# Layer 0's background adaLN sums: two of eight k tiles moved from VectorE to TensorE, and a new pace

## The chip, the cores and the metric

The kernel runs on one core of one Trainium2 chip. Its time is the device time of one execution in microseconds. A core has TensorE (PE, the matmuls; PEld are its weight loads), VectorE (DVE), ScalarE (ACT), GpSimd (POOL) and SyncE (SP), which here issues every load. The engines run side by side, each through its own queue in order, and wait for one another by semaphores.

## The reference

Two layers of a diffusion trunk run over 256 context tokens and 256 latent tokens, 1024 channels wide. For each layer:

```
sh1, sc1, ga1, sh2, sc2, ga2 = split(silu(c) @ mod_w + mod_b, 6)     # adaLN, one vector per stream
h = rms_norm(x) * g1 * (1 + sc1) + sh1
lx, ly, gq, ..., bg = split(h @ w_in)
y1, y2, y3 = rglru(lx, ly), gla(gq, gk, gv, gr, gz), gqa(aq, ak, av)
x = x + ga1 * ((sigmoid(bg1)*(y1@wb1) + sigmoid(bg2)*(y2@wb2) + sigmoid(bg3)*(y3@wb3)) @ w_out)
x = x + ga2 * (relu((rms_norm(x)*g2*(1+sc2) + sh2) @ w1)**2 @ w2)
```

`mod_w` is 1024 x 6144 in each layer. The product `silu(c) @ mod_w` has only two rows, one for the context and one for the latent stream, and it gives the 48 columns of 128 that the kernel keeps in `modT`.

## The kernel before, in words

All activations lie with channels on the partitions, in eight k tiles of 128 channels by 512 tokens. A weight tile (512 KB) is loaded by SP into one of three `wraw` buffers, split by ACT (`wh`, L200) and DVE (`wl`, L201) into a high and a low part (three buffers of each), and used in 24 matmuls (`gemm`, L252: eight k tiles by three products). Before each k tile `gemm` calls `tick()`.

The text calls a vector sum over `mod_w` an adaLN sum. The six sixths of `mod_w` are numbered u = 0 to 5; each is done in two halves of 512 columns. For layer 0, u = 0 and 1 are done at the start (`mod_half`, straight on TensorE). The generator `mods` (L310) does u = 2 to 5, that is eight halves, behind other work. For a half it loads eight tiles t of 128 x 512 (256 KB each, L319), and for each of them multiplies t by the conditioning scalar of its partition and adds it to an accumulator, once for each of the two streams: ACT for k = 0 (L339), DVE for k = 1 to 7 (L341). What remains is a sum over 128 partitions, which `mod_cols` (L288, here called the close of a half) does on TensorE: the accumulators are multiplied by `pick`, a 128 x 32 matrix with a single column of ones, in four column strips. The result is copied, transposed and added to its bias; this last part, `turn()`, comes only when the next half is closed. So both halves of u are done once the first half of u + 1 is closed.

`mods` gives a number at each step, and the kernel's own pacing clock (L206 to L231) decides at which `tick()` the next step is written into the program: every matmul advances this clock by its columns / 2400 (four times that for plain f32), so a gemm of 512 tokens counts 5.12 units and one of 256 tokens 2.56; a step is due the given number of units after the one before. `need(l, u)` (L245) writes all the steps that are missing until u is done, at once, without matmuls between them.

The stretch in question, in program order: `spawn(mods(0, range(2, 6), ...))` (L916); eleven `merge` calls of two gemms each at 512 tokens; `need(0, 2)` (L924); eight out-projection gemms on tokens 0 to 255, each followed by a `residual` on DVE (L933); the norm statistics of that half; `need(0, 3, 4)` (L953) and `norm_apply` of that half; eight out-projection gemms on tokens 256 to 511, statistics and `norm_apply` again; the first five tiles of `up` for each half of the tokens, three for all 512; `need(0, 5)`; then `mods(1, ...)` is spawned for layer 1.

`tmp()` tiles of 128 x 512, which the loads, the accumulators and the norms share, come from a pool of 10 buffers. The compiler's list scheduler orders each engine's queue; `tc.high_priority(n)` moves an instruction up by n places in it (300 for the loads of `mods`, 800 for the weights and for the norms).

Of the kernel before, what the change touches and what calls it, by code (L numbers as in the profile page):

```python
# [23 lines left out]
KT = 8  # L24
# [13 lines left out]
GZP, G0P = 2, 6  # L38
AHEAD = 800
L_SM, L_PT = 4.0, 1.5  # L40
M_A, M_K, M_S = 300, 3.0, 2.0
NDVE = (0, 2, 5)
NL = 2
O_LX, O_LY, O_GQ, O_GK, O_GV, O_GR, O_GZ = 0, 1024, 2048, 2560, 3072, 4096, 5120
# [60 lines left out]
def trunk_kernel(ctx: ExitStack, tc: tile.TileContext, out: bass.AP, d: dict):  # L105
# [17 lines left out]
    def tmp():  # L123
        return t2.tile([128, 512], F32, name="t2")
# [4 lines left out]
    def tmp1(dt=F32, shape=(128, 256)):  # L129
        return t1.tile(list(shape), dt, name="t1")  # L130
# [10 lines left out]
    def mx():  # L141
        return ps_mx.tile([128, 512], F32, name="mx")
# [6 lines left out]
    cs = const.tile([128, KT, 32], F32, name="cs")  # L149
# [14 lines left out]
    pick = const.tile([128, 2, 32], F32, name="pick")  # L164
# [4 lines left out]
    def pc(l, name, a=0, n=None):  # L169
        lo, hi = PCOLS[name]  # L170
        return par[:, l, lo + a:hi if n is None else lo + a + n]
# [38 lines left out]
    def mm(o, a, b, **kw):  # L210
        clock[0] += b.shape[-1] * (4 if b.dtype == F32 else 1) / 2400
        P.matmul(o, a, b, **kw)  # L212

    def tp(o, a):
        clock[0] += a.shape[-1] * 2 / 2400
        P.transpose(o, a, ident)  # L216
# [16 lines left out]
    def spawn(gen):  # L233
        tasks.append([clock[0], gen])

    def finish(done=lambda: not tasks):

        while not done():
            t = min(tasks, key=lambda t: t[0])
            clock[0] = max(clock[0], t[0])  # L240
            step(t)
# [3 lines left out]
    def need(l, *us):  # L245
        finish(lambda: all((l, u) in done for u in us))
# [41 lines left out]
    def mod_cols(l, n, terms, nk, dsts):  # L288

        ps = mx()  # L290
        for k in range(nk):
            w, r = terms(k)
            for j in range(4):
                mm(ps[32 * j:32 * j + 32, :n], w, r(n * j), start=k == 0, stop=k == nk - 1)
        sb = tmp1()
        S.copy(sb[:, :n], ps[:, :n])
        yield 0.0
        pt = mx()
        m = n // 128
        for i in range(m):  # L300
            tp(pt[:, 128 * i:128 * i + 128], sb[:, 128 * i:128 * i + 128])

        src = pt[:, :n].rearrange("p (i j b) -> p j i b", i=m, j=4)[:, :, :, 0:2]
        q = 4 // len(dsts)
        for h, o in enumerate(dsts):
            dst = modT[l][:, o:o + q * m, :].rearrange("p (j i) b -> p j i b", j=q)
            bia = pc(l, "modb", o, q * m).rearrange("p (j i) -> p j i", j=q).unsqueeze(3).to_broadcast([128, q, m, 2])
            V.tensor_tensor(dst, src[:, q * h:q * h + q], bia, op=ALU.add)

    def mods(l, us, pace):  # L310

        halves = [(u, j) for u in us for j in range(2)]

        def load(u, j, k):
            with tc.high_priority(M_A):
                t = tmp()
                nc.sync.dma_start(t, d["mod_w"][l, u][:, k, 512 * j:512 * j + 512])  # L319
            return t  # L320

        def turn():
            if last:
                for _ in last[0]:
                    pass
                if last[2]:
                    done.add((l, last[1]))

        last = None
        for u, j in halves:  # L330
            bs = (0, 1) if l == 0 or u < 2 else (1,)
            acc = [tmp() for _ in bs]
            nx = load(u, j, 0)
            for k in range(KT):
                t, nx = nx, load(u, j, k + 1) if k + 1 < KT else None
                for a, b in zip(acc, bs):
                    c = cs[:, k, b:b + 1]
                    if k == 0:
                        S.activation(a, t, AF.Copy, scale=c)  # L339
                    else:  # L340
                        V.scalar_tensor_tensor(a, t, c, a, op0=ALU.mult, op1=ALU.add)  # L341
                yield pace
            yield M_S
            g = mod_cols(l, 128, lambda i, acc=acc, bs=bs: (pick[:, bs[i], :], lambda c: acc[i][:, c:c + 128]),
                         len(bs), (4 * u if j == 0 else 8 + 4 * u,) if u < 2 else (8 * u + 4 * j,))
            next(g)
            turn()
            last = g, u, j
        yield pace
        turn()  # L350
# [110 lines left out]
    for l in range(NL):  # L461
# [305 lines left out]
        def merge(b, i, yh, yl):  # L767
            pb = gemm(weight(l, "br", b, i), yh, yl, c0)
            pg = gemm(weight(l, "in", O_BG + 1024 * b + 128 * i), hh, hl, c0)
            g = gtmp()  # L770
            S.activation(g[:, c0:], pg, AF.Tanh, scale=0.5)  # L771
            if b == 0:
                V.scalar_tensor_tensor(m[:, i, :], g[:, c0:], 1.0, pb, op0=ALU.add, op1=ALU.mult)
            else:
                V.scalar_tensor_tensor(g[:, c0:], g[:, c0:], 1.0, pb, op0=ALU.add, op1=ALU.mult)
                V.tensor_tensor(m[:, i, :], m[:, i, :], g[:, c0:], op=ALU.add)
            if b == 2:
                split_to(mh[:, i, c0:], ml[:, i, c0:], m[:, i, :])
# [34 lines left out]
        for t, ps in gemm_tok(l, O_AK, hh, hl, range(4)).items():  # L813
# [4 lines left out]
            a = tmp1()  # L818
# [25 lines left out]
        def gqa_q(j):  # L844

            qT = []
            ssq = sm.tile([128, 4, 4 - t0], F32, name="ssq")
            qss = {}
            for t, pq in gemm_tok(l, O_AQ + 512 * j, hh, hl, range(t0, 4)).items():
                for g in range(2):  # L850
                    ps = pq[:, 256 * g:256 * g + 256]
                    q = tmp1()
                    for a in range(2):
                        S.activation(q[:, 128 * a:128 * a + 128], ps[:, 128 * a:128 * a + 128], AF.Square,
                                     accum_out=ssq[:, 2 * g + a, t - t0:t - t0 + 1])
                    if t < 2:
                        S.copy(q, ps)
                    else:
                        rope(q, ps, 0, t - 2)
                    qss[g, t] = q  # L860
            for g in range(2):
                for a in range(2):
                    pt = mx()
                    for t in range(t0, 4):
                        P.transpose(pt[:, 128 * t:128 * t + 128], qss[g, t][:, 128 * a:128 * a + 128], ident)
                    q = tmp()
                    if not last:
                        S.activation(q[:, :256], pt[:, :256], AF.Copy, scale=pc(l, "qg"))
                    S.copy(q[:, 256:], pt[:, 256:])
                    qT.append(q)  # L870
            rs = sm.tile([128, 4, 4 - t0], F32, name="rsq")
            rsqrt(rs.rearrange("p a b -> p (a b)"), ssq.rearrange("p a b -> p (a b)"), 1.0, 128.0 * EPS)
            return qT, rs
# [31 lines left out]
        for st_ in QORD[l]:  # L905
            if st_ == "q":
                qs[len(qs)] = gqa_q(len(qs))
            elif st_ in "01":
                for g in ((0, 1), (2, 3)):
                    spawn(attend(int(st_), g, *qs[int(st_)]))  # L910
            elif st_ == "f":
                finish()
            elif st_ == "m":
                merge(1, next(mi), y2h, y2l)
            elif st_ == "u" and l == 0:
                spawn(mods(0, range(2, 6), M_K))  # L916
        if l:
            finish()
        mh, ml = ytiles("yh")
# [52 lines left out]
        for c in range(5):  # L972
            if c < 4:
                hid[c] = ytiles(("yh", "yl")[c % 2])
                n = NSPL if c == 0 and not last else 0
                for a, b in halves:
                    for i in range(n):
                        up(c, i, a, b)
                for i in range(n, 8):
                    up(c, i, c0, T)  # L980
            if c == 0:
                need(l, 5)
            if c == 4 and not last:
                need(1, 0, 1)
                hn1 = norm_mul(l + 1, 1)
                for a, b in halves[::-1]:
                    for i in range(8):
                        down(3, i, a, b)
                    with tc.high_priority(NHP):
                        norm_apply(l + 1, 1, x, a, b, norm_stats(x, a, b), hn1, range(8))  # L990
            elif c > 0:
                for i in range(8):
                    down(c - 1, i, c0, T)
                    if c == 4:
                        nc.sync.dma_start(out[:, i, :], x[:, i, 256:])
            if l == 0 and c == 0:
                spawn(mods(1, range(5), 1.5 * M_K))
        x1 = x


# [101 lines left out]
```

## Time and profile before

| | |
|---|---|
| median of 3 runs | 1927.91 us (1926.07 to 1928.13) |
| profiled execution, its own time | 1926.13 us |
| its span, first to last instruction | 1924.3 us |
| PE, DVE, ACT busy | 95%, 66%, 48% of the span |
| mean granted TensorE clock | 0.98 of full |

An engine's busy share is an average over the whole span. Where TensorE is busy without a break, what the other engines do is hidden; where it is idle, the profile names what ended the wait.

### The profile page before, as it was taken

How to read it: one execution, taken by the hardware profiler on the slowest of the kernel's cores; microseconds unless marked ns; L12 is line 12 of the kernel's file. 1: busy time of each engine (PE TensorE's matmuls, PEld its weight loads, DVE VectorE, ACT ScalarE, POOL GpSimd, SP SyncE). 2: the span in 40 equal slices, each digit the busy share in tenths (PEclk: the TensorE clock that was granted, in tenths of full speed). 3: DMA queues.
4: the chain of work that ended last, by engine and by line, in shares of the span. 5: the costliest groups of instructions: out<-in, count | busy, mean ns of one | idle time of the engine just before them, and what ended most of it. 6: DMA issues, size and time to landing. Idle time of an engine off the chain costs nothing.

```text
span 1924.3 us, 27716 instructions
## 1 busy us (share of the span) xinstructions
PE 1819.8 (95%) x10696; PEld 1544.4 (80%) x10696; DVE 1273.0 (66%) x2137; ACT 926.4 (48%) x1586; POOL 58.0 (3%) x88
## 2 busy tenths in 40 slices
PE   5998999999999999779999999996999999999999
PEld 4765778887777888778888889764888878999999
DVE  5677764445566984889854448787765677566665
ACT  3778544343443333454332325877654554445442
POOL 1000000000000000010000000000000000000000
PEclk9999999999999999879999999998999999999999
DMA  9322223222221653847643236531433333664654
GB/s 313 99 74 69 68 71 97 76 90 77 66 66 45 224 170 124 271 130 235 209 133 99 93 94 191 159 124 62 129 120 114 123 115 98 240 182 148 186 180 150
DMA packets 91619, 255.66 MB, mean 133 GB/s; under 512 B 9184, under 2 KB 20576, under 8 KB 91488
## 3 DMA queue, kind: packets, MB, share of 16 engines
q1 hardware_dynamic: 91488, 253.90, 41.6%
q8 instruction: 84, 1.38, 0.3%
q14 instruction: 47, 0.39, 0.1%
HBM read 252.82 MB, written 1.05 MB: 132 GB/s over the span
## 4 chain that ended last, share of the span: by engine, by line
PE 58%; issue 30%; DVE 6%; ACT 4%; POOL 1%; DMA 1%; SPq 0%; POOLq 0%; DVEq 0%; ACTq 0%
PE mm L212 49%; PE mx L212 2%; PE mx L744 1%; PE mx L725 1%; DVE wl L201 1%; ACT wh L200 1%; DVE t L341 1%; PE mx L216 1%; PE mx L699 1%; PE mx L510 1%; DMA t<-mod_w 1%; DVE lru L530 0%; PE mx L701 0%; DVE lru L529 0%; ACT lru L614 0%
## 5 line engine op out<-in xcount | busy, mean ns | idle before, releaser
L201 DVE TENSOR_TENSOR wl<-wraw,wh 128x1024 fp32r<-128x1024 f32 x365 | 445.9, 1224 | 297.7 <-ACT wh L200 294.5
L200 ACT CAST wh<-wraw 128x1024 fp32r<-128x1024 f32 x363 | 380.1, 1049 | 539.5 <-PE mm L212 464.2
L212 PE MATMUL mm<-hh,wh 128*128 128x512 f32 (+1 forms) x1448 | 500.3, 346 | 12.7 <-DVE big L933 6.1
L212 PE MATMUL mm<-hl,wh 128*128 128x512 f32 (+1 forms) x1448 | 496.4, 343 | 0.0
L212 PE MATMUL mm<-hh,wl 128*128 128x512 f32 (+1 forms) x1448 | 495.6, 342 | 0.0
L212 PEld LDWEIGHTS mm<-hh,wh 128*128 128x128 f32 x1448 | 276.3, 191 | 46.4 <-issue 9.6
L212 PEld LDWEIGHTS mm<-hl,wh 128*128 128x128 f32 x1448 | 276.0, 191 | 32.6 <-issue 3.5
L212 PEld LDWEIGHTS mm<-hh,wl 128*128 128x128 f32 x1448 | 275.8, 191 | 31.7 <-issue 1.4
L212 PE MATMUL mm<-yh,wh 128*128 128x512 f32 (+1 forms) x640 | 225.2, 352 | 3.3 <-DVE big L933 3.3
L212 PE MATMUL mm<-yh,wl 128*128 128x512 f32 (+1 forms) x640 | 225.0, 352 | 0.0
L212 PE MATMUL mm<-yl,wh 128*128 128x512 f32 (+1 forms) x640 | 223.3, 349 | 0.0
L212 PE MATMUL mm<-yp,wh 128*128 128x256 f32 x1024 | 190.6, 287 | 3.8 <-ACT g L771 2.3
L212 PEld LDWEIGHTS mm<-yp,wh 128*128 128x128 f32 x1024 | 161.1, 193 | 6.0 <-ACT g L771 2.5
L341 DVE SCALAR_TENSOR_TENSOR t<-t,cs,t 128x512 f32<-128x512 f32 x210 | 149.3, 752 | 12.7 <-DMA t<-mod_w 9.0
L212 PE MATMUL mm<-yp,wl 128*128 128x256 f32 x512 | 146.4, 286 | 0.8 <-DVE wl L201 0.8
L212 PEld LDWEIGHTS mm<-yh,wh 128*128 128x128 f32 x640 | 122.4, 191 | 18.7 <-DVE big L933 3.6
L212 PEld LDWEIGHTS mm<-yh,wl 128*128 128x128 f32 x640 | 122.1, 191 | 15.2 <-issue 0.5
L212 PEld LDWEIGHTS mm<-yl,wh 128*128 128x128 f32 x640 | 122.1, 191 | 14.9 <-issue 0.5
L212 PE MATMUL mm<-wh,hh 128*128 128x512 f32 x288 | 115.6, 401 | 18.5 <-ACT t L637 18.1
L212 PE MATMUL mm<-wl,hh 128*128 128x512 f32 x288 | 115.1, 400 | 2.3 <-DVE wl L201 2.3
L212 PE MATMUL mm<-wh,hl 128*128 128x512 f32 x288 | 114.4, 398 | 0.0
L933 DVE SCALAR_TENSOR_TENSOR big<-mm,modT,big 128x256 f32<-128x256 f32 x96 | 44.1, 481 | 89.0 <-PE mm L212 88.9
(223 smaller groups left out, 2223.9 us busy)
## 6 DMA issues: line engine op xcount, KB each, us to landing
wraw<-wt SPq DMA_DIRECT2D x365, 512.0 KB, 3.6
t<-mod_w SPq DMA_DIRECT2D x144, 256.0 KB, 3.9
modw<-mod_w SPq DMA_DIRECT2D x6, 2048.0 KB, 14.3
big<-xt SPq DMA_DIRECT2D x8, 512.0 KB, 5.2
gw<-lruw SPq DMA_DIRECT2D x16, 256.0 KB, 3.5
out<-big SPq DMA_DIRECT2D x8, 128.0 KB, 1.9
t<-glaw SPq DMA_DIRECT2D x8, 96.0 KB, 3.1
t<-ropeg SPq DMA_DIRECT2D x2, 256.0 KB, 2.7
```

Source lines behind the costliest of these rows:

```text
L200: S.copy(wh, r)
L201: (G if lo == "G" else V).tensor_tensor(wl, r, wh.bitcast(F32), op=ALU.subtract)
L212: P.matmul(o, a, b, **kw)
L216: P.transpose(o, a, ident)
L341: V.scalar_tensor_tensor(a, t, c, a, op0=ALU.mult, op1=ALU.add)
L510: P.matmul(pg, gw[:, 2 * dd + q, :], xc, start=True, stop=True)
L699: P.matmul(psc[:, c], en[:, c], em[:, c], start=True, stop=True)
L725: P.matmul(pu[:, :256], kt[:, 128 * t:128 * t + 128], v_[t], start=True, stop=True)
L744: P.matmul(po[:, :256], a, b, start=j == 0, stop=j == len(mm) - 1)
L933: V.scalar_tensor_tensor(x[:, i, c], ps[:, 256 * s - a:256 * s - a + 256], s0[:, i, s:s + 1], x[:, i, c], op0=ALU.mult, op1=ALU.add)
```

## The change

For layer 0, u = 2 to 5, only k = 0 to 5 of a half are summed on ACT and DVE. The tiles of k = 6 and 7 are loaded as before and kept as they are until the close, where TensorE multiplies them by their conditioning columns `cs[:, k, :]` (128 x 32, two columns used) into the same PSUM strips as the accumulators. The steps of k = 6 and 7 give nothing to the pacing clock. The pace of a step is 2.8 units in place of 3.0; that of layer 1 is 4.5 as before (1.5 x 3.0).

```diff
-M_A, M_K, M_S = 300, 3.0, 2.0
+M_A, M_S = 300, 2.0
...
-    def mods(l, us, pace):
+    def mods(l, us, pace, nd=KT):
...
             acc = [tmp() for _ in bs]
+            terms = [(pick[:, b, :], a) for a, b in zip(acc, bs)]
             nx = load(u, j, 0)
             for k in range(KT):
                 t, nx = nx, load(u, j, k + 1) if k + 1 < KT else None
+                if k >= nd:
+                    terms.append((cs[:, k, :], t))
+                    continue
                 for a, b in zip(acc, bs):
...
             yield M_S
-            g = mod_cols(l, 128, lambda i, acc=acc, bs=bs: (pick[:, bs[i], :], lambda c: acc[i][:, c:c + 128]),
-                         len(bs), (4 * u if j == 0 else 8 + 4 * u,) if u < 2 else (8 * u + 4 * j,))
+            g = mod_cols(l, 128, lambda i, terms=terms: (terms[i][0], lambda c: terms[i][1][:, c:c + 128]),
+                         len(terms), (4 * u if j == 0 else 8 + 4 * u,) if u < 2 else (8 * u + 4 * j,))
...
-                spawn(mods(0, range(2, 6), M_K))
+                spawn(mods(0, range(2, 6), 2.8, KT - 2))
...
-                spawn(mods(1, range(5), 1.5 * M_K))
+                spawn(mods(1, range(5), 4.5))
```

## Rows read from the trace of the kernel before

**Rows 1.** The page, part 1: busy time, share, instructions.
```profile
PE 1819.8 (95%) x10696; PEld 1544.4 (80%) x10696; DVE 1273.0 (66%) x2137; ACT 926.4 (48%) x1586; POOL 58.0 (3%) x88
```

**Rows 2.** Windows: PE, PEld, DVE, ACT, POOL busy (count), granted clock, DMA share, GB/s.
```profile
636.00:784.20 148.20, 148.20 (x807) 125.48 (x805) 109.28 (x152) 51.86 (x72) 0.00 (x0) 1.00 0.56 183
784.20:804.30 20.10, 19.83 (x173) 19.03 (x171) 15.91 (x25) 8.21 (x11) 0.70 (x1) 1.00 0.85 277
804.30:824.30 20.00, 3.02 (x35) 1.14 (x34) 18.40 (x35) 5.96 (x12) 2.52 (x3) 0.59 0.53 186
824.30:850.00 25.70, 19.62 (x133) 18.53 (x134) 22.95 (x46) 12.51 (x29) 3.15 (x4) 0.77 0.46 144
850.00:870.00 20.00, 20.00 (x160) 20.00 (x160) 17.82 (x35) 15.71 (x33) 1.92 (x3) 0.94 0.57 181
```

**Rows 3.** Timeline of PE around 804 us: start, duration, instruction, idle before and releaser.
```profile
803.95 0.28 PE L212 MATMUL mm<-yl,wh 128*128 128x256 f32 x1
804.07 0.28 PE L212 MATMUL mm<-yh,wl 128*128 128x256 f32 x1
806.47 0.43 PE L212 MATMUL mx<-t,pick 128*32 128x128 f32 x8 [2.12 <-DVE t L341]
808.18 0.65 PE L212 MATMUL mx<-t,pick 128*32 128x128 f32 x8 [1.02 <-DVE t L341]
819.41 1.23 PE L212 MATMUL mx<-t,pick 128*32 128x128 f32 x16 [10.57 <-DVE t L341]
824.30 0.58 PE L212 MATMUL mm<-yh,wh 128*128 128x256 f32 x1 [3.27 <-DVE big L933]
```

**Rows 4.** Windows of line 341 alone: DVE busy (count), granted clock, DMA share, GB/s.
```profile
636.00:784.20 148.20, 47.89 (x70) 1.00 0.56 183
720.00:740.00 20.00, 0.00 (x0) 1.00 0.31 91
784.20:804.30 20.10, 7.03 (x11) 1.00 0.85 277
804.30:824.30 20.00, 14.47 (x20) 0.59 0.53 186
824.30:850.00 25.70, 8.53 (x12) 0.77 0.46 144
```

**Rows 5.** The page, part 5: count, busy us, mean ns, idle before.
```profile
L341 DVE SCALAR_TENSOR_TENSOR t<-t,cs,t 128x512 f32<-128x512 f32 x210 | 149.3, 752 | 12.7 <-DMA t<-mod_w 9.0
```

**Rows 6.** Groups of PE by shape, 804.1 to 870 us.
```profile
L212 PE MATMUL mm<-hl,wh 128*128 128x256 f32 x80 | 24.0, 300 | 0.0
...
L212 PE MATMUL mm<-yh,wh 128*128 128x256 f32 x9 | 3.5, 391 | 3.3 <-DVE big L933 3.3
```

**Rows 7.** Timeline of PE: closes of halves 1, 4 and 5, and what follows the fifth.
```profile
665.19 0.64 PE L212 MATMUL mx<-t,pick 128*32 128x128 f32 x16
...
752.08 0.64 PE L212 MATMUL mx<-t,pick 128*32 128x128 f32 x16
...
787.15 0.64 PE L212 MATMUL mx<-t,pick 128*32 128x128 f32 x16
787.72 0.33 PE L216 MATMUL mx<-ident,t 128*128 128x128 f32 x1
```

**Rows 8.** Waits of the SP queue, 800 to 870 us: total us, times, longest.
```profile
SPq L319 <- POOL t L409: 14.5, 1, 14.5
```

**Rows 9.** The page, part 6: load, queue, count, KB, median us from issue to landing.
```profile
wraw<-wt SPq DMA_DIRECT2D x365, 512.0 KB, 3.6
t<-mod_w SPq DMA_DIRECT2D x144, 256.0 KB, 3.9
```

**Rows 10.** Windows as in rows 2, at the border of layers 0 and 1.
```profile
1160.00:1180.00 20.00, 19.87 (x164) 19.46 (x163) 13.37 (x24) 9.25 (x13) 0.70 (x1) 1.00 0.59 175
1180.00:1200.00 20.00, 19.98 (x166) 19.98 (x167) 19.92 (x36) 14.00 (x28) 2.94 (x4) 1.00 0.64 205
1200.00:1220.00 20.00, 19.07 (x128) 16.89 (x127) 16.09 (x33) 14.43 (x27) 3.62 (x5) 1.00 0.60 193
```

## The prediction, on record before the run

> **What bounds the kernel now.** I read the page first: TensorE is busy for 95% of the span [rows 1]. So work taken from another engine gains only where PE stands still, and work given to PE costs its full length everywhere else. I then cut the stretch in which layer 0's adaLN sums run into windows [rows 2]. From 636 to 784 us PE never stops; there VectorE's 109 us of work are hidden. From 804.3 to 824.3 PE works 3.0 of 20 us, from 824.3 to 850 it loses another 6.1, and the granted clock falls to 0.59 and 0.77, a mixture of the full level (2.4 GHz) and the half one (1.2 GHz), before it is back at 0.94 and then full. The timeline says what PE waits for: closes of halves, which wait for line 341, 2.12 + 1.02 + 10.57 us, and then a gemm that waits 3.27 us for an eviction on DVE [rows 3]. DVE is busy 18.4 of those 20 us, 14.5 of them on line 341 [rows 2, 4]. So here, and only here, the background sums set the end.
>
> Why then? The windows of line 341 show a gap: 70 instructions (five halves of 14) are over before 784 us, none ran between 720 and 740, and then 43 more fall due at once [rows 4]. That is the pacing clock. In units of 2400 columns, 22 merge gemms of 5.12 and eight out gemms of 2.56 stand before `need(0, 3, 4)`: 133.12 units. Ticks come every three matmuls, 0.64 units in merges, so a pace of 3.0 lands on the fifth tick, 3.2, and 2.0 on the fourth, 2.56. The first half closes at 8 x 3.2 + 2.56 = 28.16, the next ones 26.2 to 26.9 later (a close counts 1.7 units itself), the fourth at 107.5, the fifth not before 133. As u = 4 is only done when u = 5's first half is closed, `need` writes the rest of the fifth half and all of the sixth and seventh at one spot. The trace agrees with this order: closes 1 and 4 run at 665.19 and 752.08, 29 us apart each, the fifth only at 787.15 [rows 7].
>
> **The pace and the skipped steps.** A pace of 2.8 also lands on 3.2 in merges; what shortens a half is that it has six steps and not eight. A close now counts 16 x 0.213 = 3.4 units, more than 2.8, so the step behind it follows at once. First close: 6 x 3.2 + 2.56 = 21.76; then one every 5 x 3.2 + 2.56 = 18.56. The fifth is at 96.0, the sixth at 114.2. In the out gemms ticks come every 0.32, 2.8 becomes 2.88 and 2.0 becomes 2.24, so the seventh comes 5 x 2.88 + 2.24 = 16.64 later, at 130.9. That is 2.2 units, under one gemm, ahead of `need(0, 3, 4)` at 133.12: it finds everything done and writes nothing. The eighth is at 147.5, before the out projection ends at 153.6. Here 2.8 matters: a half late by 2.3 units would put a burst back.
>
> **What the stall costs now.** After 804.07 the next matmul was due at 804.19; 870 us is 65.8 us later. What PE did in between at full rate: matmuls of 256 columns, three groups of 80 like the first of [rows 6] and three of 9 like the second, 267 x 0.12 us (the spacing of 803.95 and 804.07 [rows 3]) = 32.0; three closes at 0.57 (787.15 to the next instruction [rows 7]) = 1.7; twelve small matmuls and transposes of the norms and turns, 1.4 if also at 0.12. Together 35.1, so 30.7 us are lost: 23.1 of idle time [rows 2], the rest at the lower clock. All of it can come back, because with no idle time the clock had stayed full up to 804.3.
>
> **What VectorE is spared.** Two k tiles by two streams by eight halves = 32 instructions x 0.752 us [rows 5] = 24.1 us. Where PE is full, this is worth nothing. In 784.2 to 870 it decides: DVE was busy 75.1 us there (sum of [rows 2]), about 32.3 on line 341 (the three windows of [rows 4] and three instructions more at 0.75), 42.8 on the rest. With the sixth and seventh halves moved ahead of 784 us, into a stretch where DVE had 148.2 - 109.3 = 39 us free and needs 20 x 0.752 = 15 more for them but 20 x 0.752 = 15 less for the first five, there remain 42.8 + 7.5 (eighth half) + 2.3 (layer 1's first) = 52.6 us. PE needs 20.1 + 35.1 = 55 for the same. DVE fits, at 95%, barely.
>
> **What TensorE gets.** Two more terms a half: eight matmuls, each two PE instructions as now (16 for two accumulators [rows 7]), so 16 more at 0.57 us: 8 x 0.57 = 4.6 us, all on the path, for PE is full there. From below it is 0, if the closes fell into idle time; from above, each of the 16 after the other with the length of the whole present group, which nothing in [rows 7] supports. I take 4.6, as operands have the same shapes. The Trainium skill, FP8 and Floating Point Precision, TensorE Precision Notes, has true FP32 take four passes through the array. By that rule eight matmuls of 128 columns one after another are an estimated 1.7 us at 2.4 GHz, the sum would have 13.7 in place of 4.6, and the time would be 9 us longer; the present group, equally eight f32 matmuls, takes 0.57 us [rows 7], so the strips overlap and the row decides.
>
> **What is held longer.** A half keeps four of the ten buffers (two accumulators, two raw tiles) until its close, not two. Two halves may be ahead of PE, not four. At 18.56 units a half, some 20 us, its ten DVE instructions (7.5 us) and eight loads (3.9 us each to landing, overlapping [rows 9]) fit, so PE should find closes ready. The 64 loads are the same on the same queue; the last two of a half are asked for without a step between them, 2 to 6 units before the close if they came no earlier than written, but the loads of the first five halves ran tens of us ahead of their closes (line 341 was done with them by 720 [rows 4], the fifth close is at 787 [rows 7]). Layer 1's pace is unchanged.
>
> **What is left of the stall.** From below: at the border of the layers the same 256-token gemms and norms run with few sums, and PE loses 0.13 + 0.02 + 0.93 = 1.1 us in 60 although DVE reaches 19.9 of 20 [rows 10]. From above: DVE as full as now (75.1 of 85.8 us, 87.5%) with the seventh half late as well, (52.6 + 7.5) / 0.875 = 68.7 against 55, 13.7 us. Without that half it is 60.1 - 55 = 5. I take 4, between the border's 1.1 and 5.
>
> Sum on the profiled time: 1926.1 - 30.7 + 4.6 + 4 = 1904. The median of before lies 1.8 above its profiled execution; I give it half of that: 1905.
>
> **The rivals.**
> Partial: the stall shrinks but VectorE stays the bound from 784 to 850 us. For it: 95% of full, norms and evictions in one strict queue, buffers that let the seventh half start only after the fifth close. Against it: [rows 10]. With 8 to 14 us left, and some clock lost behind it, 1909 to 1920.
>
> No gain: the gap at 804 is really the chain of evictions and norms (the last wait in [rows 3] is on L933), and the sums only fill it. Then 1926.1 + 4.6 = 1930.7, or up to 8 less. Against it: the three waits on line 341 carry 13.7 of 17.
>
> Slower: a load of a k tile reaches the head of SP's queue before its buffer is free and holds the weight loads behind it. It happened once: 14.5 us for one tile, freed by POOL [rows 8], and now buffers come free only at closes. At most five weights lie split or loaded ahead; at 24 x 0.12 = 2.88 us a gemm that is 14.4 us, less 3.6 for landing [rows 9] and some 2.3 for the split, so a hold above 8.5 us starves PE in the out projection, and above 21 in the merges, longer than a half. Three holds of 18 us, at closes six to eight, cost 29, and the time would be 1929 to 1935. It decides from about 17 us a hold. The Trainium skill, DMA: Bandwidth & Descriptors, Anatomy of one DMA, says that a semaphore wait happens on the issuing sequencer before dispatch; by that rule the trace agrees with its 14.5 us, and the queue does stop.
>
> **How the numbers follow.** Forecast (1898 to 1909) 0.60; partial 0.25; no gain 0.06; slower 0.06; better still, closes hidden and nothing left (under 1898), 0.03. The range 1898 to 1918 leaves out the end of the partial case, no gain and slower. Faster by over 0.2% (about what three runs here can tell apart): 0.60 + 0.25 + 0.03 = 0.88; within 0.2%, most of no gain: 0.05; slower 0.07.
>
> **What would show it.** Closes about 20 us apart from near 658 us on, seven before the out projection's first half ends, each about 1.1 us long; line 341 with 178 instructions in place of 210; PE without a gap over 3 us between 784 and 850, clock 1.00. Wrong would be: closes that wait for a load; a long wait of line 319 on the SP queue with PE idle behind it; or DVE still at 19 of 20 us with a gemm waiting for L933.

## The result, and the profile after

The changed kernel takes 1907.5 us (median of 4, 1904.2 to 1908.7) against 1927.7 us: a ratio of 0.9894, 95% interval 0.9877 to 0.9911. It is 20 us faster, and 2.5 us off the forecast of 1905. The profiled execution took 1904.2 us, 21.9 less than the one of before.

The page of the changed kernel, parts 1 and 5 (L345 is what L341 was):

```profile
PE 1817.4 (96%) x10824; PEld 1542.1 (81%) x10824; DVE 1252.9 (66%) x2105; ACT 925.0 (49%) x1586; POOL 57.1 (3%) x88
...
L345 DVE SCALAR_TENSOR_TENSOR t<-t,cs,t 128x512 f32<-128x512 f32 x178 | 127.2, 746 | 24.6 <-DMA t<-mod_w 15.4
```

TensorE has 128 instructions more, VectorE 32 sums fewer, as written in the diff. Where the time came from is seen in the windows of the changed kernel (columns as in [rows 2]):

```profile
784.20:804.30 20.10, 19.94 (x176) 19.37 (x165) 17.21 (x34) 11.97 (x25) 3.74 (x5) 1.00 0.62 187
804.30:824.30 20.00, 16.64 (x156) 15.45 (x155) 16.80 (x33) 8.90 (x16) 2.44 (x4) 1.00 0.54 172
824.30:850.00 25.70, 24.91 (x199) 24.26 (x199) 23.00 (x41) 19.51 (x39) 1.29 (x2) 1.00 0.76 258
```

From 804.3 to 824.3 us PE works 16.6 us in place of 3.0, and the granted clock is 1.00 where it was 0.59 [rows 2]. The timeline of its PE shows the closes of halves 1, 3 and 7 (two lines each: accumulators, then raw tiles), the transpose behind the third, the one long gap, the start of the eighth close's two parts, and the first matmul of 512 tokens of `up`:

```profile
658.43 0.64 PE L212 MATMUL mx<-t,pick 128*32 128x128 f32 x16
658.89 0.62 PE L212 MATMUL mx<-t,cs 128*32 128x128 f32 x16
...
700.41 0.64 PE L212 MATMUL mx<-t,pick 128*32 128x128 f32 x16
700.87 0.62 PE L212 MATMUL mx<-t,cs 128*32 128x128 f32 x16
701.42 0.33 PE L216 MATMUL mx<-ident,t 128*128 128x128 f32 x1
...
783.48 0.65 PE L212 MATMUL mx<-t,pick 128*32 128x128 f32 x16
783.94 0.62 PE L212 MATMUL mx<-t,cs 128*32 128x128 f32 x16
...
808.90 0.36 PE L212 MATMUL mm<-yh,wh 128*128 128x256 f32 x1 [2.75 <-DVE big L937]
809.78 0.42 PE L212 MATMUL mx<-t,pick 128*32 128x128 f32 x8
...
812.06 0.43 PE L212 MATMUL mx<-t,pick 128*32 128x128 f32 x8
...
848.46 0.40 PE L212 MATMUL mm<-hh,wh 128*128 128x512 f32 x1
```

Closes come some 21 us apart, and none waits. Gone are the three waits on the sums and the 3.27 us behind them [rows 3], and a later wait of 6.08 us that rows 3 do not reach; in their place stands one of 2.75 us. The later wait too was put down to line 933, but what stood ahead of that eviction in the kernel before were five sums without a break:

```profile
839.98 3.40 DVE L341 SCALAR_TENSOR_TENSOR t<-t,cs,t 128x512 f32<-128x512 f32 x5
843.29 0.48 DVE L933 SCALAR_TENSOR_TENSOR big<-mm,ga,big 128x256 f32<-128x256 f32 x1
...
843.92 0.55 PE L212 MATMUL mm<-hh,wh 128*128 128x256 f32 x1 [6.08 <-DVE big L933]
```

The matmul at 848.46 stood at 869.97 in the kernel before: 21.5 of the 21.9 us are gained up to there. A close with raw tiles lasts 700.41 to 701.42, 1.01 us, against 0.57 [rows 7]; the added 16 instructions cost 0.44.

### The profile page after: what moved, and what is told of

It reads as the page before. It is cut to its first block, busy times and chain, and to the rows that moved or that the text cites. A ratio compares the mean times of both kernels' runs of the same rounds, so it can differ in the third digit from the quotient of the medians.

```text
span 1902.5 us, 27909 instructions
## 1 busy us (share of the span) xinstructions
PE 1817.4 (96%) x10824; PEld 1542.1 (81%) x10824; DVE 1252.9 (66%) x2105; ACT 925.0 (49%) x1586; POOL 57.1 (3%) x88
## 4 chain that ended last, share of the span: by engine, by line
PE 44%; issue 40%; DVE 7%; ACT 6%; POOL 1%; DMA 0%; SPq 0%; POOLq 0%; ACTq 0%; DVEq 0%
PE mm L212 35%; PE mx L212 2%; PE mx L514 1%; PE mx L748 1%; DVE wl L201 1%; PE mx L729 1%; ACT wh L200 1%; DVE lru L534 1%; ACT lru L515 1%; ACT lru L618 1%; DVE lru L533 1%; DVE lru L536 1%; PE mx L703 1%; PE mx L216 1%; ACT lru L519 1%
## 5 line engine op out<-in xcount | busy, mean ns | idle before, releaser
L345 DVE SCALAR_TENSOR_TENSOR t<-t,cs,t 128x512 f32<-128x512 f32 x178 | 127.2, 746 | 24.6 <-DMA t<-mod_w 15.4
```

## The experiments

Every run is compared with the kernel before on the same chip, by ratio and its 95% interval; the changed kernel stands at 0.9894. All edits are made to the changed kernel. The question was what exactly had cost the 30 us: where the steps are written, how many VectorE instructions there are, or something else.

**1. All eight k tiles on VectorE, pace 1.9.**

```diff
-                spawn(mods(0, range(2, 6), 2.8, KT - 2))
+                spawn(mods(0, range(2, 6), 1.9, KT))
```

> All eight k tiles on VectorE as before, but a pace of 1.9: by the pacing clock the halves close at 17.9, 34.6, 51.2, 67.8, 84.5, 101.1, 117.4 and 133.4 units, so need(0, 3, 4) at 133.1 finds nothing to write. Theory 'order' (the loss was the burst of 19 steps written at one spot): the 30.7 us come back without the 4.6 us of extra matmuls, less 4 to 9 us that remain because VectorE keeps its 24 us: a median of 1901 to 1907. Rival 'VectorE work' (the gain comes from the 32 instructions taken from VectorE): 1920 or more.

Measured: 1898.3 us, 0.9858 (0.9844 to 0.9871). It is faster than the changed kernel, with no sum taken from VectorE, and below the 1901 to 1907 of "order": the 4 to 9 us that VectorE's work was still to cost are not there, as PE idles only 1.4 us from 784.2 to 850 us. The waits of its PE, 620 to 880 us:

```profile
PE mm L212 <- DVE g L970: 0.6, 1, 0.6
PE mx L392 <- DVE t L391: 0.6, 2, 0.4
```

and two of its windows in the merges:

```profile
660.00:680.00 20.00, 20.00 (x103) 16.22 (x102) 20.00 (x30) 6.21 (x9) 0.00 (x0) 1.00 0.75 237
680.00:700.00 20.00, 20.00 (x103) 16.20 (x102) 19.76 (x29) 7.95 (x11) 0.00 (x0) 1.00 0.75 238
```

VectorE is full there, and so is PE: here a full VectorE costs nothing, as TensorE has all that it needs. What is gone is the stall after 804 us.

**2. Two k tiles on TensorE, pace 3.3.**

```diff
+                spawn(mods(0, range(2, 6), 3.3, KT - 2))
```

> The changed kernel with a pace of 3.3, which lands on the sixth tick (3.84 units): the seventh half closes only at need(0, 3, 4), which has six of its seven steps to write. VectorE is spared the same 24 us. Order: a third of the burst (6 of 19 steps) is back, some 10 us: 1914 to 1919. VectorE work: as the changed kernel, 1905 to 1910.

Measured: 1912.8 us, 0.9934 (0.9921 to 0.9946), 6.8 us more than with 3.0 (run 4). That is between the two forecasts, nearer to that of "order". The stall is back in part, though VectorE has its 32 instructions fewer. Its PE, and its windows:

```profile
817.14 0.55 PE L212 MATMUL mm<-yh,wh 128*128 128x256 f32 x1 [7.51 <-DVE big L937]
```
```profile
804.30:824.30 20.00, 12.49 (x108) 11.82 (x107) 18.60 (x37) 10.39 (x24) 0.89 (x2) 0.74 0.50 169
```

**3. All on VectorE, pace 2.8: the pace alone.**

```diff
+                spawn(mods(0, range(2, 6), 2.8, KT))
```

> All eight k tiles on VectorE and only the pace of 2.8 in place of 3.0: both land on 3.2 units in the merges, so the closes hardly move and need(0, 3, 4) still writes 17 steps (19 before). Order and VectorE work: 1923 to 1929, no gain to speak of. Rival 'pace' (the smaller number by itself brings the gain): 1917 or less.

Measured: 1923.3 us, 0.9980 (0.9972 to 0.9989): some 4 us, a small gain. Its PE still waits 11.40 us for the sums:

```profile
814.69 0.66 PE L212 MATMUL mx<-t,pick 128*32 128x128 f32 x8 [11.40 <-DVE t L345]
```

**4. Two k tiles on TensorE, pace 3.0: without the new pace.**

```diff
+                spawn(mods(0, range(2, 6), 3.0, KT - 2))
```

> The changed kernel with the old pace of 3.0: the seventh half closes at 132.5 units and not at 130.9, still ahead of need(0, 3, 4) at 133.1. Order and VectorE work: 1906 to 1910, the same as the changed kernel. Pace: 1914 or more.

Measured: 1906.0 us, 0.9894 (0.9879 to 0.9909), the ratio of the changed kernel. The pace of 2.8 does nothing that 3.0 doesn't.

**5. The price of a raw term.** A raw term is a k tile that goes into the close as it was loaded. Here each close gets two further ones, against zeros; they add nothing to the sum.

```diff
+            if nd < KT:
+                terms += [(zero, a) for _, a in terms[-2:]]
```

> The changed kernel with two more terms in each close of layer 0's background halves: the raw tiles of k = 6 and 7 once more, against a 128 x 32 tile of zeros (it adds nothing to the result). No instruction of VectorE, no load and no close's place changes. If a pair of raw terms costs its 0.55 us on the path of TensorE, as the prediction's 4.6 us say, 8 x 0.55 = 4.4 us are added: 1910 to 1913. Rival (closes are hidden in what is left of the stall): 1905 to 1908.

Measured: 1909.5 us, 0.9916 (0.9903 to 0.9930), 0.0022 or 4.2 us above the changed kernel; the two intervals overlap by a little, and the time lies between the two forecasts. Its timeline prices the group itself:

```profile
703.99 0.64 PE L215 MATMUL mx<-t,pick 128*32 128x128 f32 x16
704.45 0.62 PE L215 MATMUL mx<-t,cs 128*32 128x128 f32 x16
704.88 0.62 PE L215 MATMUL mx<-t,zero 128*32 128x128 f32 x16
705.43 0.33 PE L219 MATMUL mx<-ident,t 128*128 128x128 f32 x1
```

From 703.99 to 705.43 are 1.44 us for three groups, 0.43 for each one added, 3.5 us for eight closes.

**6. Pace 3.0, all on VectorE, transposes earlier.** A miss.

```diff
+                if l == 0 and k == 2:
+                    turn()
+                    last = None
                 yield pace
...
-            turn()
+            if l:
+                turn()
...
+                spawn(mods(0, range(2, 6), 3.0, KT))
```

> The kernel before (all on VectorE, pace 3.0), but the transposes of a half are written at the third step of the next half and not behind its close, so that need(0, 3, 4) has 13 steps to write in place of 19 (the seventh half's accumulation is no longer among them but for three steps). Order: 6 of 19 steps of 30 us are saved, some 9: 1914 to 1920. Rival 'VectorE work': nothing is taken from VectorE, so 1924 to 1928.

Measured: 1925.4 us, 0.9992 (0.9983 to 1.0001), no gain, although fewer steps are written at `need(0, 3, 4)`. Its PE waits less at that spot and more behind it:

```profile
808.04 0.66 PE L212 MATMUL mx<-t,pick 128*32 128x128 f32 x8 [3.19 <-DVE t L345]
...
819.98 0.58 PE L212 MATMUL mm<-yh,wh 128*128 128x256 f32 x1 [8.39 <-DVE big L941]
...
856.07 0.36 PE L212 MATMUL mm<-hh,wh 128*128 128x256 f32 x1 [2.40 <-ACT g L973]
...
865.01 0.47 PE L212 MATMUL mm<-hh,wh 128*128 128x512 f32 x1 [2.96 <-DVE g L974]
```

So fewer steps at one spot brought nothing. VectorE still had the same 42 sums of halves six to eight to do after 785 us; done later, they hold up `up` in place of the out projection.

**7. Two k tiles on TensorE, pace 4.0.**

```diff
+                spawn(mods(0, range(2, 6), 4.0, KT - 2))
```

> The changed kernel (two k tiles on TensorE, VectorE spared its 24 us) with a pace of 4.0: need(0, 3, 4) has 13 steps to write again. Order: as the run with the early turn, which also has 13, plus 4.4 us for the closes, 1917 to 1924. VectorE work: as the changed kernel, 1905 to 1910.

Measured: 1917.9 us, 0.9957 (0.9944 to 0.9969), inside the range of "order". Spared instructions alone bring not even half of the gain when the halves come late.

**8. All on VectorE, pace 1.2.**

```diff
+                spawn(mods(0, range(2, 6), 1.2, KT))
```

> All eight k tiles on VectorE at a pace of 1.2: the halves would close at 12.8, 24.3 ... 93.4 units, far ahead of need(0, 3, 4). Order (only the missing steps at that spot count): 1897 to 1901, as with 1.9. Rival 'throughput' (VectorE, ten and a half us a half at the least beside its other work, can't follow a close every 11.5 units, so that TensorE waits at the closes): 1904 or more.

Measured: 1902.4 us, 0.9877 (0.9864 to 0.9891), some 4 us more than with 1.9, though the intervals overlap by a little. That is between the two forecasts. The stall is as absent as there, but closes come before VectorE has finished, and the scheduler cuts them in two, with gemm matmuls between the parts:

```profile
677.55 0.43 PE L212 MATMUL mx<-t,pick 128*32 128x128 f32 x8
677.91 0.33 PE L216 MATMUL mx<-ident,t 128*128 128x128 f32 x1
...
679.79 0.43 PE L212 MATMUL mx<-t,pick 128*32 128x128 f32 x8
680.15 0.50 PE L212 MATMUL mm<-hh,wl 128*128 128x512 f32 x1
```

A part of eight instructions takes 0.36 us, two of them 0.72, the uncut sixteen 0.57. The Trainium skill, TensorEngine Tiling (Array Packing), Key Properties, says that changing the tiling mode drains TensorE; the trace agrees in that two visits cost 0.72 us where one of the same work costs 0.57. What this does to the merges is read from their 528 matmuls of 512 tokens, of which these are the first and the last, in this run, in run 1 and in the kernel before:

```profile
635.18 0.40 PE L212 MATMUL mm<-yh,wh 128*128 128x512 f32 x1
...
765.31 0.39 PE L212 MATMUL mm<-hh,wl 128*128 128x512 f32 x1
```
```profile
635.53 0.39 PE L212 MATMUL mm<-yh,wh 128*128 128x512 f32 x1
...
760.18 0.39 PE L212 MATMUL mm<-hh,wl 128*128 128x512 f32 x1
```
```profile
635.15 0.39 PE L212 MATMUL mm<-yh,wh 128*128 128x512 f32 x1
...
758.07 0.39 PE L212 MATMUL mm<-hh,wl 128*128 128x512 f32 x1
```

They take 122.92 us in the kernel before with four closes among them, 124.65 in run 1 with six, so a whole close costs some 0.87 us with its transposes and what is lost around it. Run 8, with all eight, would be at 126.4, but takes 130.13: the cut closes and a wait of 0.26 us account for 3.7 of the 4 us.

After these eight a second theory stood against "order": **backlog**. What costs is the VectorE work of layer 0's sums that is still open at 785 us, when out projection, norms and the first `up` tiles need VectorE nearly all the time. Run 6 speaks for it, but only after the fact, so two runs (9 and 10) were made for which the two theories forecast changes of opposite sign.

**9. The kernel before, asked earlier.** All on VectorE, pace 3.0, and one line:

```diff
-        need(l, 2)
+        need(l, *((2, 3, 4) if l == 0 else (2,)))
...
+                spawn(mods(0, range(2, 6), 3.0, KT))
```

> The kernel before (all k tiles on VectorE, pace 3.0, late transposes), but what need(0, 3, 4) asks for is asked for already at need(0, 2), eight gemms of 256 tokens earlier: some 25 steps are now written at one spot, more than the 19 of before, ahead of the out projection and not in it. Theory 'order' as put so far (a burst written at one spot stops TensorE by its length): no gain or a loss, 1924 to 1940. Theory 'backlog' (what costs is the VectorE work of the sums that is still open when the out projection and the norms need VectorE, from 785 us on; before that spot VectorE has some 40 us free): 28 of its 45 instructions there are gone, 1899 to 1909.

Measured: 1897.8 us, 0.9853 (0.9836 to 0.9869). A longer burst, eight gemms earlier, brings the whole gain, 1 us more than "backlog" forecast; all 42 sums are gone from behind 785 us, not the 28 forecast. Its closes five to seven stand together, and none waits:

```profile
760.66 0.64 PE L212 MATMUL mx<-t,pick 128*32 128x128 f32 x16
...
761.50 0.65 PE L212 MATMUL mx<-t,pick 128*32 128x128 f32 x16
...
762.74 0.65 PE L212 MATMUL mx<-t,pick 128*32 128x128 f32 x16
```

VectorE had done those sums in the time in which it stood idle before [rows 4], as its windows in the kernel before and here show (its busy time stands third, 47.56 against 71.70 us):

```profile
700.00:785.00 85.00, 84.88 (x504) 73.77 (x502) 47.56 (x65) 29.42 (x41) 0.00 (x0) 1.00 0.46 149
```
```profile
700.00:785.00 85.00, 85.00 (x529) 72.70 (x528) 71.70 (x108) 32.51 (x48) 0.00 (x0) 1.00 0.68 219
```

**10. The same with u = 5 as well.**

```diff
+        need(l, *((2, 3, 4, 5) if l == 0 else (2,)))
```

> As the run with the early need, with the two halves of u = 5 asked for there as well, some 34 steps at one spot. Order: a loss, 1930 or more. Backlog: hardly any of layer 0's sums is left after 785 us, but 35 VectorE instructions have to fit between 709 and about 765 us, so TensorE may wait up to 10 us at the last closes: 1897 to 1910.

Measured: 1901.9 us, 0.9876 (0.9861 to 0.9891). The eighth close does wait, as feared, but little:

```profile
775.85 0.42 PE L212 MATMUL mx<-t,pick 128*32 128x128 f32 x8 [0.87 <-DVE t L345]
```

**11. Two k tiles on TensorE, pace 2.5.**

```diff
+                spawn(mods(0, range(2, 6), 2.5, KT - 2))
```

> The changed kernel (two k tiles on TensorE) with a pace of 2.5, which closes its halves where the all-VectorE kernel with 1.9 closes them, or a little earlier (17.9, 33.3 ... 110.1, 125.1 units). Backlog: the stall is gone in both, so the two raw terms are only a cost, 8 x 0.44 to 0.57 us more than the 1898 of that kernel: 1900 to 1904. VectorE work (its 24 us are worth something by themselves): below 1898.

Measured: 1902.6 us, 0.9882 (0.9867 to 0.9896): 0.0024 or 4.6 us above run 1, in line with 8 x 0.44 = 3.5, though the intervals overlap. The traces agree: from the first merge matmul to the first of 512 tokens in `up` are 209.9 us here (635.21 to 845.10) and 206.4 in run 1 (635.53 to 841.93). Where the stall is gone, the raw terms are only a cost.

The windows of the sums' line alone from 620 to 785 us, all of them layer 0's, for the kernel before, the changed one, run 7 and run 1, in this order (DVE busy us, count):

```profile
620.00:785.00 165.00, 48.45 (x70) 1.00 0.54 175
```
```profile
620.00:785.00 165.00, 52.05 (x74) 1.00 0.63 202
```
```profile
620.00:785.00 165.00, 37.98 (x54) 1.00 0.55 177
```
```profile
620.00:785.00 165.00, 77.32 (x112) 1.00 0.65 211
```

Layer 0 has 112 such sums on VectorE, 80 with two k tiles on TensorE. What is left of them after 785 us, read in this way from every trace, against the ratio, and the ratio less 3.5 us where TensorE has raw terms (3.5 / 1926 = 0.0018, twice that in run 5):

| kernel | left after 785 us | ratio | less raw terms |
|---|---|---|---|
| before | 42 | 1 | 1 |
| 6 (transposes early) | 42 | 0.9992 | 0.9992 |
| 3 (pace 2.8 alone) | 38 | 0.9980 | 0.9980 |
| 7 (two on PE, 4.0) | 26 | 0.9957 | 0.9939 |
| 2 (two on PE, 3.3) | 16 | 0.9934 | 0.9916 |
| changed, and 4 | 6 | 0.9894 | 0.9876 |
| 5 (zeros added) | 6 | 0.9916 | 0.9880 |
| 11 (two on PE, 2.5) | 0 | 0.9882 | 0.9864 |
| 1, 9, 8, 10 (all on VectorE) | 0 | 0.9858, 0.9853, 0.9877, 0.9876 | the same |

Down to 16 the order is that of the count; 6 left and none no longer differ beyond the intervals. From 42 to 0 it is some 28 us, 0.67 us for each sum, near the 0.752 us that one takes [rows 5]. Neither the number of sums (112 in the two fastest kernels) nor the number of steps at one spot (run 6 against run 9) orders the ratios so.

One rival goes along with the sums: their loads come late too. Runs 3 and 7 tell the two apart. Both had issued 43 of the 64 loads of `mod_w` for layer 0 by 785 us, but 38 and 26 sums were left, and run 7 is the faster although it alone pays for raw terms. And in the kernel before, VectorE was busy for 57.3 of the 65.8 us from 784.2 to 850 [rows 2] and waited for those loads only this long (total us, times, longest):

```profile
DVE t L341 <- DMA t<-mod_w: 2.6, 4, 1.1
```

## Why the prediction was right

*The loss of 30.7 us.* Right: the kernels that leave no stall and add nothing to TensorE save 27 to 28 us (runs 9 and 1). PE still idles 1.8 and 1.4 us there from 784.2 to 850; what is missing then to 30.7, some 1.5 us, lies within the intervals. Part of it was the lower clock, and it came back with the idle time.

*The pacing clock.* Right for the closes: the first was to come near 658 us and runs at 658.43, and the seventh, worked out at 130.9 units, ahead of the 133.1 of `need(0, 3, 4)`, runs at 783.48, within the out projection's first half. But "here 2.8 matters" was wrong, though the number did not hang on it: 3.0 gives the same steps in the merges and 132.5 units for the seventh close, which is still in time (run 4); the border lies between 3.2, the fifth tick, and the 3.3 of run 2. In the changed kernel the six steps do the work, not the pace.

*The extra terms.* Right in mechanism, mis-sized: 0.44 us a close and not 0.57, 3.5 us in all and not 4.6, because 0.57 holds a fixed part (half such a group took 0.36, run 8) that a longer group does not pay again. The Trainium skill, FP8 and Floating Point Precision, TensorE Precision Notes, has true FP32 take four passes, from which the prediction estimated 1.7 us for eight matmuls one after another. The same rows refute only the "one after another": with four strips side by side the estimate is a quarter of that, 0.43 us, and each added group took 0.43 to 0.44.

*What is left.* Forecast 4 us; PE's idle time from 784.2 to 850 is now 0.16 + 3.36 + 0.79 = 4.3 us, at a clock of 1.00. The sum with measured terms, -30.7 + 3.5 + 4.3 = -22.9, stands against 21.9.

*What VectorE is spared.* The step that was only half right. The prediction's budget from 784.2 to 870 us, 52.6 us of VectorE work against 55 of TensorE, named the right quantity (measured up to the matmul at 848.46: 55.5 and 60.0), but it let 24.1 us fewer sums "decide" there. Run 1 spares none and wins more: the 39 us that VectorE had free before 784 hold the late halves whole. What decides is how many sums are left behind 785 us.

*The rivals.* No close waited for a load, and no hold of SP starved PE: the longest wait of line 319 on the SP queue from 700 to 880 us was 4.7 us, against 14.5 before [rows 8]. VectorE as the remaining bound was the nearest rival; its 2.75 us wait is the tail of it, with the eighth half's last six sums. "No gain" was held unlikely because the waits on line 341 carry 13.7 of 17 us; over the whole stretch it is 13.7 of 23.1, and 9.3 were put down to line 933. What speaks against it is the five sums ahead of the later of these two evictions, and run 9, where both waits are gone.

One thing stays open: run 10 lies 4 us above run 9, with intervals that overlap. In the traces it is 2.1 us behind at the first `up` matmul of 512 tokens, of which PE's idle time between 760 and 785 us is 1.9; the rest was not traced.

## What to carry to other kernels

Budget a background task by stretches: sum what its engine still owes when a stage begins that needs that engine, and write the task early enough that nothing is left, even if the engine then runs full under a bound that does not need it. Moving work to the engine that bounds the kernel is the dearer way to the same end; ask for the result earlier first. Here the deadline in the program (`need`) showed in the trace as idle time of the helper engine well ahead of the stall.

## What the runs showed of the hardware

A group of plain f32 matmuls in four column strips of 32 has a fixed part: 8 PE instructions took 0.36 us, 16 took 0.57, 32 took 1.01, 48 took 1.44. From 804.3 to 824.3 us the granted clock, a mixture of 2.4 and 1.2 GHz where it is below 1.00, was 1.00 with a longest gap of PE of 2.75 us (changed kernel), 0.91 with one of 2.07 (run 4), 0.74 with one of 7.51 (run 2) and 0.59 with one of 10.57 [rows 2, 3]: the longest gap alone does not order it.
